# The residual of a transformer layer kept in the result's DRAM rows, with the last norm added by accumulating DMAs

## The chip, the cores and the metric

The kernel runs on 1 core of one Trainium2 chip. The metric is the device time of the program in microseconds; lower is better. Within the core, TensorE (PE) multiplies, VectorE (DVE), ScalarE (ACT) and GpSimd (POOL) do elementwise work, and SyncE (SP) issues DMAs. Each engine takes its instructions strictly in the order of its own queue, and engines wait for each other by semaphores.

## The reference

One layer over x of 1024 tokens by 1024 channels, in float32: a mixing block and a SwiGLU feed-forward block, each with a norm before and after it and a residual around it.

```python
def rms_norm(x, g):
    y = x * lax.rsqrt(jnp.mean(x * x, axis=-1, keepdims=True) + EPS)
    return y * g

def swiglu(h, w1, w2):
    gt, up = jnp.split(h @ w1, 2, axis=-1)
    return (jax.nn.silu(gt) * up) @ w2

h = rms_norm(x, norm_mix_pre)
y = hybrid_mixer(h, ...)                  # four mixers, gates, output projection
x = x + rms_norm(y, norm_mix_post)        # the residual, here called x1
h = rms_norm(x, norm_ffn_pre)
x = x + rms_norm(swiglu(h, w_ffn_in, w_ffn_out), norm_ffn_post)
```

The hidden width of the feed-forward block is 2816. The change concerns how x1 is kept and how the last line adds it.

## The kernel before

Tokens are cut into eight tiles of 128 (rows 0 to 7 below), each 128 partitions by 1024 float32 (512 KB). Products keep float32 accuracy by splitting each operand into a high and a low part (`split`, L139 to L145: ScalarE writes `whi`, VectorE writes `wlo`) and summing three matmuls.

`second_norm` (L1088) computes the residual x1 of each tile and stores it from SyncE into a DRAM tile `x1_{tt}` (L1103, L1105), since SBUF has no room for it during the feed-forward block.

`ffn_out` (L1180) computes the second feed-forward product in three chunks of the hidden width; the third, with `final` true, has three pairs of 128 hidden rows. Each chunk is a Strassen-Winograd scheme of seven products over quadrants. Each product fills four PSUM tiles (`mm_fo`), one for each 128 tokens of a half, and takes 3 pairs times 3 matmuls of 512 columns for each: 36 matmuls. Two sets of four PSUM tiles are used in turns, `ps1` (`mm_fo0` to `mm_fo3`, numbers 1805 to 1808) and `ps2` (`mm_fo4` to `mm_fo7`, numbers 1809 to 1812). `into` (L1266) adds a finished PSUM tile to half of a row's accumulator `ya` (L1272, VectorE). The calls are written in the order of L1319 to L1322: two products, then m6, m5, m3, m7, m4.

- m6, on `ps1`, adds into the first half of rows 4 to 7; m5 goes on in the same PSUM tiles, so it can start only when VectorE has read what m6 left there.
- m3, on `ps1`, completes rows 0 to 3.
- m7, on `ps2`, completes the second half of rows 4 to 7, and m4 goes on in its PSUM tiles and completes rows 4 to 7.

`half_done` (L1278) is the last norm of half a row: the sum of squares on ScalarE (L1282), the multiplication by the norm's weight on VectorE (L1283, in place, so after the square has read), the mean on GpSimd (L1286 for the first half, L1292 for the second), then the reciprocal root on GpSimd (L1294), and for each half of the row `y * r + x1` on VectorE (L1297) and a store of 256 KB from SyncE (L1298). x1 was loaded back into an SBUF slot `x1b` at the first half (L1287 to L1289).

What sets the order: the code is written with priorities (`tc.high_priority`), and a scheduler lays every engine's queue down at build time; slots of SBUF are handed out as earlier tiles die. So an edit can move instructions that it does not name.

Of the kernel before, what the change touches and what calls it, by code (L numbers as in the profile page):

```python
# [9 lines left out]
F32 = mybir.dt.float32  # L10
F32R = mybir.dt.float32r
U8 = mybir.dt.uint8
AF = mybir.ActivationFunctionType
ALU = mybir.AluOpType
# [3 lines left out]
P = 128  # L18
S = 1024
D = 1024  # L20
NT = S // P
# [17 lines left out]
def hybrid_trunk(ctx, tc, x, w_in, w_branch, w_out, w_ffn_in, w_ffn_out, cols, gpost, gfpost,  # L39
                 abias, wst, bsr, wabd, wxbd, lvl, tril, eye, out, dbg=None):  # L40
    nc = tc.nc
    dbg = dbg or {}

    def pool(name, bufs, **kw):
        return ctx.enter_context(tc.tile_pool(name=name, bufs=bufs, **kw))
# [9 lines left out]
    dr = pool("dram", 1, space=bass.MemoryType.DRAM)  # L55
# [24 lines left out]
    def slot(name, dt=F32, w=D):  # L80
        cnt[0] += 1
        t = sp.tile([P, D], dt, tag="S", name=f"{name}_{cnt[0]}", bufs=NSLOT)
        return t[:, :w]
# [17 lines left out]
    def small(name, w):  # L101
        cnt[0] += 1
        return sm.tile([P, w], F32, tag=f"s{w}", name=f"{name}_{cnt[0]}", bufs={1: 24, 8: 8}.get(w, 4))
# [43 lines left out]
    AHEAD_DMA, AHEAD_SUM, AHEAD_OUT, AHEAD_SPLIT = 700, 400, 400, 160  # L147
# [98 lines left out]
    def rstd_of(ss, n, w):  # L246

        ms = small("ms", w)
        nc.gpsimd.tensor_scalar(ms, ss, 1.0 / n, EPS, op0=ALU.mult, op1=ALU.add)
        r = small("rstd", w)  # L250
        last[2] = nc.gpsimd.tensor_tensor(r, ms, neghalf[:, :w], op=ALU.pow)
        return r
# [4 lines left out]
    def halves(name):  # L257

        tiles = {}

        def get(k, ts):
            h = ts.start // 512
            if (h, k // 2) not in tiles:
                tiles[h, k // 2] = slot(f"{name}{h}{k // 2}", F32R)
            b = (k % 2) * 512 - h * 512
            return tiles[h, k // 2][:, b + ts.start : b + ts.stop]

        get.tiles = tiles
        return get
# [97 lines left out]
    def normed(xtile, wait=None):  # L367

        ss = small("ss", 1)
        with after(wait):  # L370
            nc.scalar.activation(junk, xtile, AF.Square, accum_out=ss)
        r = rstd_of(ss, D, 1)
        xn = slot("xn")
        nc.vector.tensor_scalar(xn, xtile, r, None, op0=ALU.mult)
        return xn

    def place_T(srcs, tt, gcol, Th, Tl):

        ts = slice(tt * P, (tt + 2) * P)
        for k in range(0, KT, 2):  # L380
            ps = psmx("tr")
            for v in range(2):
                for u in range(2):
                    nc.tensor.transpose(ps[:, v * 256 + u * P : v * 256 + (u + 1) * P],
                                        srcs[u][:, (k + v) * P : (k + v + 1) * P], ident)
            gs = [cv[:, gcol + k + v : gcol + k + v + 1] for v in range(2)]
            pvs = [ps[:, v * 256 : (v + 1) * 256] for v in range(2)]
            for v in range(2):
                g, pv = gs[v], pvs[v]
                last[0] = nc.scalar.activation(Th(k + v, ts), pv, AF.Copy, scale=g)  # L390
                first_T.append(last[0])
            for v in range(2):
                g, pv = gs[v], pvs[v]
                last[1] = nc.vector.scalar_tensor_tensor(Tl(k + v, ts), pv, g, Th(k + v, ts).bitcast(F32),
                                                         op0=ALU.mult, op1=ALU.subtract)
# [675 lines left out]
    h2h, h2l, x1s = halves("h2h"), halves("h2l"), {}  # L1071
# [16 lines left out]
    def second_norm(th):  # L1088
        xt, xns = {}, {}

        def load(tt):
            xt[tt] = slot("xt2")
            with tc.high_priority(AHEAD_X):
                return nc.sync.dma_start(xt[tt], x[tt * P : (tt + 1) * P, :])

        def residual(tt):
            y = ys.pop(tt)
            ss = small("yss", 1)
            nc.scalar.activation(junk, y, AF.Square, accum_out=ss)
            r = rstd_of(ss, D, 1)  # L1100
            nc.vector.scalar_tensor_tensor(y, y, r, gp, op0=ALU.mult, op1=ALU.mult)
            nc.vector.tensor_tensor(xt[tt], xt[tt], y, op=ALU.add)
            x1s[tt] = dr.tile([P, D], F32, name=f"x1_{tt}")  # L1103
            with tc.issue_after(loads[-1].ins):
                nc.sync.dma_start(x1s[tt], xt[tt])  # L1105

        t0 = 4 * th
        loads = [load(t0 + u) for u in range(4)]
        for u in range(5):
            if u < 4:  # L1110
                residual(t0 + u)
                yield
            if u >= 1:
                xns[u - 1] = normed(xt.pop(t0 + u - 1))
                yield
                if u % 2 == 0:
                    place_T([xns.pop(u - 2), xns.pop(u - 1)], t0 + u - 2, C_GFFN, h2h, h2l)
                    yield
# [61 lines left out]
    def ffn_out(chunk, first, final):  # L1180
        n = len(chunk)
        pairs_ = []
        for i, p in enumerate(chunk):
# [13 lines left out]
            for nm, t in (("A", a), ("B", w)):  # L1197
                for u in range(2):
                    for h in range(2):
                        r, c_ = (h, u) if nm == "A" else (u, h)  # L1200
# [75 lines left out]
        early, xts_ = {}, {}  # L1276

        def half_done(tt, c_, second):  # L1278

            y = yacc[tt][:, halfs[c_]]  # L1280
            ss = small("yss", 1)
            nc.scalar.activation(junk[:, :512], y, AF.Square, accum_out=ss)  # L1282
            nc.vector.tensor_tensor(y, y, gf[:, halfs[c_]], op=ALU.mult)  # L1283
            if not second:
                early[tt] = small("ms0", 1)
                nc.gpsimd.tensor_scalar(early[tt], ss, 1.0 / D, EPS, op0=ALU.mult, op1=ALU.add)  # L1286
                xts_[tt] = slot("x1b")  # L1287
                with tc.high_priority(AHEAD_OUT):
                    nc.sync.dma_start(xts_[tt], x1s[tt])  # L1289
                return  # L1290
            ms = small("ms", 1)
            nc.gpsimd.tensor_scalar(ms, ss, 1.0 / D, early[tt], op0=ALU.mult, op1=ALU.add)  # L1292
            r = small("rstd", 1)
            nc.gpsimd.tensor_tensor(r, ms, neghalf[:, :1], op=ALU.pow)  # L1294
            for cs in (halfs[1 - c_], halfs[c_]):
                xt = xts_[tt][:, cs]
                nc.vector.scalar_tensor_tensor(xt, yacc[tt][:, cs], r, xt, op0=ALU.mult, op1=ALU.add)  # L1297
                nc.sync.dma_start(out[tt * P : (tt + 1) * P, cs], xt)  # L1298
# [4 lines left out]
        def into_last(r, c_, second):  # L1303

            ev = into(r, c_, (r, c_) == (0, 1))

            def evl(t, ps):
                ev(t, ps)
                if final:
                    half_done(4 * r + t, c_, second)  # L1310

            return evl
# [22 lines left out]
    yacc = [slot(f"ya{t}") for t in range(NT)]  # L1335
# [64 lines left out]
```

## Time and profile before

| | |
|---|---|
| median of 3 runs | 1540.26 us (1538.35 to 1542.23) |
| the profiled execution: its own time | 1538.24 us |
| its span in the trace | 1536.4 us |
| PE busy | 1500.5 us, 98% |
| VectorE busy | 1024.8 us, 67% |
| ScalarE busy | 567.6 us, 37% |
| GpSimd busy | 393.9 us, 26% |
| DMAs of the hardware queue | 190.16 MB, 35.5% of 16 engines' span |

The span runs from the first to the last instruction of the trace; 1.84 us of the execution's own time lie around it. A busy PE does not tell what sets the end: in the last stretch of the program the multiplications are over, and the queues of the other engines set it. The views for that are the busy time of each engine by stretch, the instructions in order of time, and the chain of work that ended last. In the lists of instructions a row gives the start, the time until the result is there, the engine, the line, what is written from what, the count, and in brackets the idle time of the engine before it with what ended it. Instructions of one engine overlap a little, so a row's time is some 0.08 us longer than the distance to the next start.

### The profile page before, as it was taken

The numbers are of one execution on the slowest core, as the hardware profiler recorded it, in microseconds if no ns is written. First come the engines' busy times: TensorE is split into PE (matmuls) and PEld (weight loads), VectorE is DVE, ScalarE is ACT, GpSimd is POOL, SyncE is SP. The second block draws the span as 40 slices with busy tenths as digits, with TensorE's granted clock in tenths as the row PEclk, the third lists the DMA queues.
The fourth block names the chain that finished last, engine by engine and source line by source line (L and its number), as shares of the span: only waits on it lengthen the run. The fifth ranks groups of instructions, "written<-read, shape, count | busy, mean of one in ns | idle before, by whom it ended". The sixth has DMA issues, their size and how long they took to land.

```text
span 1536.4 us, 20562 instructions
## 1 busy us (share of the span) xinstructions
PE 1500.5 (98%) x7890; PEld 1253.4 (82%) x7890; DVE 1024.8 (67%) x1569; ACT 567.6 (37%) x942; POOL 393.9 (26%) x343
## 2 busy tenths in 40 slices
PE   8999999999999999999999999999999999999996
PEld 7988888888888878766899978888888888787875
DVE  5986674444459567888765695555555556869898
ACT  6433343333330343344335542222222222553543
POOL 2075333333200100223533223433333330000003
PEclk9999999999999999999999999999999999999998
DMA  6424333333462146563225412222222236630203
GB/s 228 157 85 157 110 110 110 110 110 113 140 213 97 63 157 239 210 243 118 69 97 192 177 64 76 82 85 88 81 84 83 83 110 229 228 112 28 82 22 144
DMA packets 108547, 191.48 MB, mean 125 GB/s; under 512 B 6432, under 2 KB 65440, under 8 KB 108448
## 3 DMA queue, kind: packets, MB, share of 16 engines
q1 hardware_dynamic: 108448, 190.16, 35.5%
q8 instruction: 62, 1.02, 0.3%
q14 instruction: 37, 0.30, 0.1%
HBM read 136.66 MB, written 53.48 MB: 124 GB/s over the span
## 4 chain that ended last, share of the span: by engine, by line
PE 87%; DVE 9%; ACT 2%; issue 1%; POOL 1%; DMA 0%; DVEq 0%; SPq 0%; ACTq 0%; POOLq 0%
PE mm_w L218 16%; PE mm_w L216 16%; PE mm_w L217 16%; PE mm_fo L1239 3%; PE mm_fo L1240 3%; PE mm_fo L1238 3%; PE mm_gate L216 3%; PE mm_gate L217 2%; PE mm_gate L218 2%; PE mm_proj L216 2%; PE mm_proj L217 2%; PE mm_proj L218 2%; PE mm_wo L217 1%; PE mm_wo L218 1%; PE mm_wo L216 1%
## 5 line engine op out<-in xcount | busy, mean ns | idle before, releaser
L142 DVE TENSOR_TENSOR wlo_ws<-s,whi_ws 128x1024 fp32r<-128x1024 f32 x76 | 109.1, 1435 | 54.4 <-ACT whi_ws L141 54.4
L361 DVE TENSOR_TENSOR u<-u,mm_w 128x512 f32<-128x512 f32 x38 | 26.1, 687 | 174.8 <-PE mm_w L218 174.8
L141 ACT CAST whi_ws<-s 128x1024 fp32r<-128x1024 f32 x76 | 80.1, 1054 | 150.2 <-PE mm_w L217 138.3
L1239 PE MATMUL mm_fo<-wlo_fo,whi_fo 128*128 128x512 f32 x308 | 120.2, 392 | 1.3 <-DVE wlo_fo L142 1.3
L1240 PE MATMUL mm_fo<-whi_fo,wlo_fo 128*128 128x512 f32 x308 | 120.2, 392 | 0.1
L324 POOL TENSOR_TENSOR s<-raw_pj 128x512 f32<-128x512 f32 x38 | 57.0, 1500 | 195.7 <-DMA raw_pj<-in_w_in 186.8
L324 POOL TENSOR_TENSOR s<-raw_fu 128x512 f32<-128x512 f32 x19 | 39.7, 2090 | 222.5 <-DMA raw_fu<-in_w_ffn_in 222.5
L1238 PE MATMUL mm_fo<-whi_fo 128*128 128x512 f32 x308 | 91.8, 392 | 4.6 <-DVE ya L1272 3.3
L345 ACT COPY m<-mm_w 128x512 f32<-128x512 f32 x38 | 22.3, 587 | 155.4 <-PE mm_w L218 141.6
L141 ACT CAST whi_fo<-af 128x512 fp32r<-128x512 f32 x66 | 41.2, 624 | 96.4 <-PE mm_fo L1240 76.7
L218 PE MATMUL mm_wo<-whi_wo,ml 128*128 128x256 f32 x256 | 72.4, 284 | 1.2 <-DVE ml L927 1.2
L217 PE MATMUL mm_wo<-wlo_wo,mh 128*128 128x256 f32 x256 | 72.2, 284 | 1.4 <-DVE wlo_wo L142 1.4
L1238 PEld LDWEIGHTS mm_fo<-whi_fo 128*128 128x128 f32 x308 | 57.9, 189 | 19.1 <-DVE ya L1272 4.1
L216 PE MATMUL mm_wo<-whi_wo,mh 128*128 128x256 f32 x256 | 71.5, 284 | 0.6 <-ACT whi_wo L141 0.6
L1239 PEld LDWEIGHTS mm_fo<-wlo_fo,whi_fo 128*128 128x128 f32 x308 | 58.2, 189 | 13.8 <-DVE wlo_fo L142 1.7
L1240 PEld LDWEIGHTS mm_fo<-whi_fo,wlo_fo 128*128 128x128 f32 x308 | 58.2, 189 | 12.6 <-DVE wlo_fo L142 0.4
L1286 POOL TENSOR_SCALAR ms<-yss 128x1 f32<-128x1 f32 x8 | 5.6, 698 | 228.0 <-ACT junk L1282 227.7
L218 PE MATMUL mm_w<-T2h,wlo_ws 128*128 128x512 f32 x152 | 59.3, 390 | 2.2 <-DVE wlo_ws L142 2.2
L217 PE MATMUL mm_w<-T2l,whi_ws 128*128 128x512 f32 x152 | 59.1, 389 | 0.0
L216 PE MATMUL mm_w<-hTh,whi_wa 128*128 128x512 f32 x152 | 59.1, 389 | 0.0
L217 PE MATMUL mm_w<-hTl,whi_wa 128*128 128x512 f32 x152 | 59.1, 389 | 0.0
L216 PE MATMUL mm_w<-T2h,whi_ws 128*128 128x512 f32 x152 | 59.1, 389 | 0.0
(388 smaller groups left out, 4609.2 us busy)
## 6 DMA issues: line engine op xcount, KB each, us to landing
raw_pj<-in_w_in SPq DMA_DIRECT2D x19, 1024.0 KB, 5.9
gt<-st_g SPq DMA_DIRECT2D x22, 512.0 KB, 4.8
raw_fg<-in_w_ffn_in SPq DMA_DIRECT2D x11, 1024.0 KB, 5.1
raw_fu<-in_w_ffn_in SPq DMA_DIRECT2D x11, 1024.0 KB, 5.5
af<-act SPq DMA_DIRECT2D x22, 512.0 KB, 3.9
wf<-in_w_ffn_out SPq DMA_DIRECT2D x18, 512.0 KB, 6.4
xt<-in_x SPq DMA_DIRECT2D x16, 512.0 KB, 7.6
raw_wo<-in_w_out SPq DMA_DIRECT2D x8, 1024.0 KB, 5.1
```

The costliest lines, as they stand in the source:

```text
L141: nc.scalar.copy(hi, src)
L142: return nc.vector.tensor_tensor(lo, src, hi.bitcast(F32), op=ALU.subtract)
L216: nc.tensor.matmul(ps, lhsT=lh(k), rhs=rh(k), start=(not more and k == 0), stop=False, skip_group_check=more)
L217: nc.tensor.matmul(ps, lhsT=lh(k), rhs=rl(k), start=False, stop=False, skip_group_check=more)
L218: nc.tensor.matmul(ps, lhsT=ll(k), rhs=rh(k), start=False, stop=(k == n - 1), skip_group_check=more)
L324: last_sum[0] = nc.gpsimd.tensor_tensor(out_, x0, x1_, op=op)
L345: nc.scalar.copy(m1, p1)
L361: nc.vector.tensor_tensor(u2, u2, p3, op=ALU.add)
L1238: nc.tensor.matmul(ps, lhsT=hi[:, ts], rhs=hi[:, 512:1024], start=start, stop=False, skip_group_check=more)
L1239: nc.tensor.matmul(ps, lhsT=hi[:, ts], rhs=lo[:, 512:1024], start=False, stop=False, skip_group_check=more)
L1240: nc.tensor.matmul(ps, lhsT=lo[:, ts], rhs=hi[:, 512:1024], start=False, stop=stop, skip_group_check=more)
L1286: nc.gpsimd.tensor_scalar(early[tt], ss, 1.0 / D, EPS, op0=ALU.mult, op1=ALU.add)
```

## The change

The stored residual of rows 0 to 6 goes straight into the result's own rows in DRAM; row 7 keeps its DRAM tile. At the end the rows 0 to 6 are not loaded back: ScalarE multiplies the whole row by the reciprocal root in place, and GpSimd issues one DMA of 512 KB that adds it to what stands in the result. Row 7 is done as before.

```diff
-            x1s[tt] = dr.tile([P, D], F32, name=f"x1_{tt}")
+
+            x1s[tt] = dr.tile([P, D], F32, name=f"x1_{tt}") if tt == NT - 1 else out[tt * P : (tt + 1) * P, :]
...
-                xts_[tt] = slot("x1b")
-                with tc.high_priority(AHEAD_OUT):
-                    nc.sync.dma_start(xts_[tt], x1s[tt])
+                if tt == NT - 1:
+                    xts_[tt] = slot("x1b")
+                    with tc.high_priority(AHEAD_OUT):
+                        nc.sync.dma_start(xts_[tt], x1s[tt])
                 return
...
+            if tt < NT - 1:
+                nc.scalar.activation(yacc[tt], yacc[tt], AF.Copy, scale=r)
+                nc.gpsimd.dma_start(x1s[tt], yacc[tt], accum_op=ALU.add)
+                return
             for cs in (halfs[1 - c_], halfs[c_]):
```

Up to the last chunk of `ffn_out` no engine's queue changes but for the target of seven stores. From there on the scheduler lays the queues down differently. Lines from 1104 on are one to six higher in the changed kernel: L1272 is L1273, L1282 is L1283, L1283 is L1284, L1292 is L1294, L1294 is L1296; the new scaling is L1298, the new DMA L1299.

VectorE, at the read of m6's first PSUM tile (`ya4` from `mm_fo0`, entry 1428 of its queue), before:

```order
L142 TENSOR_TENSOR wlo_fo_1872_12640<-wf_1795_12219,whi_fo_1871_12639 128x512
L1272 TENSOR_TENSOR ya3_1672_10990<-ya3_1672_10990,mm_fo7_1812_12246 128x512
L1283 TENSOR_TENSOR ya0_1669_10987<-ya0_1669_10987,gfpost_1668_10985 128x512
L142 TENSOR_TENSOR wlo_fo_1855_12538<-af_1794_12216,whi_fo_1855_12537 128x512
L142 TENSOR_TENSOR wlo_fo_1855_12538<-wf_1796_12220,whi_fo_1855_12537 128x512
L142 TENSOR_TENSOR wlo_fo_1856_12544<-af_1798_12224,whi_fo_1856_12543 128x512
L142 TENSOR_TENSOR wlo_fo_1856_12544<-wf_1800_12228,whi_fo_1856_12543 128x512
L1283 TENSOR_TENSOR ya1_1670_10988<-ya1_1670_10988,gfpost_1668_10985 128x512
L1272 TENSOR_TENSOR ya4_1673_10991<-ya4_1673_10991,mm_fo0_1805_12239 128x512
```

The same read in the changed kernel, now entry 1440:

```order
L1284 TENSOR_TENSOR ya2_1671_10982<-ya2_1671_10982,gfpost_1668_10978 128x512
L142 TENSOR_TENSOR wlo_fo_1874_12629<-wf_1803_12228,whi_fo_1873_12628 128x512
L1284 TENSOR_TENSOR ya3_1672_10983<-ya3_1672_10983,gfpost_1668_10978 128x512
L142 TENSOR_TENSOR wlo_fo_1874_12629<-af_1801_12224,whi_fo_1873_12628 128x512
L142 TENSOR_TENSOR wlo_fo_1886_12697<-af_1794_12209,whi_fo_1885_12696 128x512
L142 TENSOR_TENSOR wlo_fo_1886_12697<-wf_1796_12213,whi_fo_1885_12696 128x512
L142 TENSOR_TENSOR wlo_fo_1889_12703<-af_1798_12217,whi_fo_1888_12702 128x512
L142 TENSOR_TENSOR wlo_fo_1889_12703<-wf_1800_12221,whi_fo_1888_12702 128x512
L142 TENSOR_TENSOR wlo_fo_1892_12709<-af_1802_12225,whi_fo_1891_12708 128x512
L142 TENSOR_TENSOR wlo_fo_1892_12709<-wf_1804_12229,whi_fo_1891_12708 128x512
L1273 TENSOR_TENSOR ya4_1673_10984<-ya4_1673_10984,mm_fo0_1805_12232 128x512
```

The read stands behind four multiplications by the weight instead of two and behind all splits of the last products; on PE all of m7 now stands ahead of m5, where before a few matmuls of m7 stood behind it.

ScalarE, its last entries in the changed kernel (`junk` rows are the squares of half a row, `ya` rows the new scalings; before, the same squares stood there alone):

```order
L1283 ACTIVATE junk_87,yss_1875_12644<-ya4_1673_10984 128x512
L1298 ACTIVATE ya3_1672_10983<-ya3_1672_10983,rstd_1865_12612 128x1024
L1283 ACTIVATE junk_87,yss_1877_12659<-ya5_1674_10985 128x512
L1283 ACTIVATE junk_87,yss_1879_12674<-ya6_1675_10986 128x512
L1283 ACTIVATE junk_87,yss_1881_12689<-ya7_1676_10987 128x512
L1283 ACTIVATE junk_87,yss_1893_12724<-ya4_1673_10984 128x512
L1283 ACTIVATE junk_87,yss_1896_12743<-ya5_1674_10985 128x512
L1298 ACTIVATE ya4_1673_10984<-ya4_1673_10984,rstd_1895_12729 128x1024
L1283 ACTIVATE junk_87,yss_1899_12762<-ya6_1675_10986 128x512
L1298 ACTIVATE ya5_1674_10985<-ya5_1674_10985,rstd_1898_12748 128x1024
L1283 ACTIVATE junk_87,yss_1902_12781<-ya7_1676_10987 128x512
L1298 ACTIVATE ya6_1675_10986<-ya6_1675_10986,rstd_1901_12767 128x1024
```

GpSimd, its last entries in the changed kernel (before, the same entries without the DMAs):

```order
L1299 DMA out_0<-ya4_1673_10984 128x1024
L1294 TENSOR_SCALAR ms_1900_12765<-yss_1899_12762,ms0_1880_12677 128x1
L1296 TENSOR_TENSOR rstd_1901_12767<-ms_1900_12765,neghalf_88 128x1
L1299 DMA out_0<-ya5_1674_10985 128x1024
L1294 TENSOR_SCALAR ms_1903_12784<-yss_1902_12781,ms0_1882_12692 128x1
L1296 TENSOR_TENSOR rstd_1904_12786<-ms_1903_12784,neghalf_88 128x1
L1299 DMA out_0<-ya6_1675_10986 128x1024
```

Each scaling on ScalarE waits for the root of its row from GpSimd, each DMA on GpSimd waits for the scaling of its row, and the mean and the root of row 7 now stand behind the DMA of row 5.

## Rows read from the trace of the kernel before

**Rows 1.** Page: span and busy time of each engine.

```profile
span 1536.4 us, 20562 instructions
PE 1500.5 (98%) x7890; PEld 1253.4 (82%) x7890; DVE 1024.8 (67%) x1569; ACT 567.6 (37%) x942; POOL 393.9 (26%) x343
```

**Rows 2.** Busy time by stretch (columns in the first row); the last row counts matmuls.

```profile
core 0: us, PE busy (x) PEld busy (x) DVE busy (x) ACT busy (x) POOL busy (x), PEclk, DMA share, GB/s
1456.70:1500.00 43.30, 39.92 (x173) 32.16 (x173) 43.29 (x72) 18.54 (x37) 3.04 (x4) 1.00 0.09 31
1509.00:1522.90 13.90, 13.88 (x62) 11.05 (x60) 13.57 (x22) 5.79 (x16) 8.83 (x14) 1.00 0.35 134
1522.90:1533.40 10.50, 0.00 (x0) 0.00 (x0) 10.44 (x17) 2.17 (x6) 5.06 (x7) 0.72 0.44 171
1494.00:1522.90 28.90, 28.88 (x128) 23.45 (x126) 27.09 (x45) 9.95 (x24) 8.83 (x14) 1.00 0.37 137
```

**Rows 3.** Instructions in order of time: PE at m5's start, and its last matmul.

```profile
1493.53 0.50 PE L1238 MATMUL mm_fo<-whi_fo 128*128 128x512 f32 x1 [1.24 <-DVE ya L1272]
1522.49 0.39 PE L1240 MATMUL mm_fo<-whi_fo,wlo_fo 128*128 128x512 f32 x1
```

**Rows 4.** Instructions in order of time: VectorE.

```profile
1456.71 0.69 DVE L142 TENSOR_TENSOR wlo_fo<-af,whi_fo 128x512 fp32r<-128x512 f32 x1 [0.63 <-ACT whi_fo L141]
1492.79 0.68 DVE L1272 TENSOR_TENSOR ya<-ya,mm_fo 128x512 f32<-128x512 f32 x1
1526.22 0.68 DVE L1272 TENSOR_TENSOR ya<-ya,mm_fo 128x512 f32<-128x512 f32 x1
1529.35 1.40 DVE L1297 SCALAR_TENSOR_TENSOR x1b<-ya,rstd,x1b 128x512 f32<-128x512 f32 x2
1531.27 2.07 DVE L1297 SCALAR_TENSOR_TENSOR x1b<-ya,rstd,x1b 128x512 f32<-128x512 f32 x3
```

**Rows 5.** Groups by line, 1509 to 1533.5 us.

```profile
L1297 DVE SCALAR_TENSOR_TENSOR x1b<-ya,rstd,x1b 128x512 f32<-128x512 f32 x16 | 11.4, 744 | 0.3 <-POOL rstd L1294 0.2
L1292 POOL TENSOR_SCALAR ms<-yss,ms 128x1 f32<-128x1 f32 x8 | 6.6, 820 | 22.3 <-ACT junk L1282 22.3
L1294 POOL TENSOR_TENSOR rstd<-ms,neghalf 128x1 f32<-128x1 f32 x8 | 4.8, 599 | 0.7
```

**Rows 6.** Instructions in order of time: ScalarE, squares.

```profile
1516.03 0.63 ACT L1282 ACTIVATE junk<-ya 128x512 f32<-128x512 f32 x1
1516.57 0.19 ACT L1282 ACTIVATION_READ_ACCUMULATOR junk<-ya 128x1 f32 x1
1516.79 0.63 ACT L1282 ACTIVATE junk<-ya 128x512 f32<-128x512 f32 x1
```

**Rows 7.** Groups by line, whole span: ScalarE on a row of 1024, and GpSimd's longest.

```profile
L371 ACT ACTIVATE junk<-xt 128x1024 f32<-128x1024 f32 x16 | 17.2, 1072 | 11.9 <-DVE xt L1102 9.2 <-DMA xt<-in_x 2.6
L494 POOL TENSOR_SCALAR g<-g 128x512 f32<-128x512 f32 x1 | 2.4, 2405 | 0.4 <-DVE g L493 0.4
```

**Rows 8.** SyncE's last stores: duration ns min, median, max; first and last start.

```profile
L1298 SPq DMA_DIRECT2D out<-x1b x16: 332/332/1055, 1511.2 to 1533.4; - x16
```

**Rows 9.** DMA issues: count, KB each, median us from issue to landing.

```profile
x<-xt SPq DMA_DIRECT2D x8, 512.0 KB, 2.7
x1b<-x SPq DMA_DIRECT2D x8, 512.0 KB, 3.7
out<-x1b SPq DMA_DIRECT2D x16, 256.0 KB, 2.0
```

## The prediction

> **What bounds the kernel now.** I read the page first, then the busy time by stretch, then the instructions in order of time of the last 80 us. By the page PE is busy 98% of the span [rows 1], so only what shortens PE's queue or what follows its last matmul can change the time. The stretches show two places where VectorE, not PE, is the late engine. From 1456.7 to 1500 us it is busy 43.29 of 43.30 us while PE has gaps, and from 1522.9 to 1533.4 us it is busy 10.44 of 10.50 us with PE done [rows 2]. In the first of them PE waits for VectorE: m5's first matmul starts at 1493.53 us after 1.24 us of idling, released by the L1272 read that VectorE started at 1492.79 us [rows 3, 4]. PE's last matmul ends at 1522.49 + 0.39 = 1522.88 us [rows 3]. VectorE's last L1297 ends at 1531.27 + 2.07 = 1533.34 us [rows 4], 10.46 us later, and the span ends at 1536.4 us, 3.06 us after that, with the last store, which was issued at 1533.4 us [rows 8]. A store of that kind lands 2.0 us after its issue [rows 9], which leaves 0.9 to 1.0 us behind the landing.
>
> **What is removed.** VectorE loses 14 of 16 instructions on L1297. Three of them in a row take 2.07 us and two 1.40 us [rows 4], so one occupies the queue 0.67 us: 14 x 0.67 = 9.4 us, all in the last VectorE-bound stretch. Seven loads of x1b and 14 stores leave SyncE. I cost them at nothing: where the loads run the DMA share is 0.09 and later at most 0.44 [rows 2], and nothing on SyncE waits behind them. The first store of x1 has the same size and the same queue place as before, so nothing there either.
>
> **The first term: PE ends later.** The removed loads also give SBUF slots back, and the scheduler lays down the last chunk differently. VectorE's read that releases m5 was entry 1428 and is entry 1440. Both queues have the same number of entries up to 1368, which is the split that started at 1456.71 us [rows 4]; from there to 1428 are 60 entries in 1492.79 - 1456.71 = 36.08 us, 0.601 us each, without a gap [rows 2]. So the read starts 12 x 0.601 = 7.2 us later, at 1500.0 us, and m5 follows 0.74 us behind it as now: 1500.75 us. In exchange all of m7 stands ahead of m5, so what is left behind it is m5, m3 and m4, 3 x 36 = 108 matmuls. 128 take 28.9 us [rows 2], so 108 take 24.4 us. The last matmul ends at 1525.15 us: **+2.3 us**. I call this time T.
>
> **The second term: the tail behind T.** The work taken from VectorE goes into two queues that are in order. ScalarE gets seven scalings of 128x1024. The trace has no such Copy; the nearest row on ScalarE reads and writes the same shape in 1.07 us [rows 7], which I take. A square takes 0.76 us from one start to the next [rows 6], a mean 0.82 and a root 0.60 us on GpSimd [rows 5]. How long GpSimd is held by issuing an accumulating DMA no row shows: SyncE's issue takes 0.33 us [rows 8], GpSimd's longest instruction of another kind 2.4 us [rows 7]; I take 1.0 us, nearer to the small one since an issue moves no data, and keep both ends.
>
> Walking the queues in their new order, in us from T (PSUM tiles come 2.04 us apart, rows 0 to 3 at -14.3 to -8.15, rows 4 to 7 at -6.1 to 0):
>
> - Row 0: square ends -12.85, root -11.45, scaling -10.4, DMA issue until -9.4. GpSimd was held, so the means and roots of rows 1 and 2 end at -8.0 and -6.6, the scalings of rows 1 and 2 at -6.95 and -5.5.
> - ScalarE takes row 3's square only now, until -4.75, though its half was there at -7.5; then row 4's first square until -4.0. GpSimd issues the DMAs of rows 1 and 2 until -4.5, row 3's root ends -3.1, its scaling -2.05.
> - Five squares follow on ScalarE: rows 5, 6, 7 first halves, rows 4 and 5 second halves, until 1.75. GpSimd, with the DMA of row 3 and three means between, has the roots of rows 4 and 5 at 2.75 and 4.15.
> - Scaling of row 4 until 3.8, square of row 6 until 4.55, scaling of row 5 until 5.6, square of row 7 until 6.35.
> - GpSimd: DMA of row 4 until 5.15, root of row 6 at 6.55, DMA of row 5 until 7.55, then row 7's mean and root until 8.95. Then VectorE's two L1297 of row 7, 0.67 + 0.74: 10.35.
>
> VectorE ended 10.46 us behind PE and now ends 10.35 us behind it: the 9.4 us it loses come back as ScalarE and GpSimd waiting for each other. Row 7's stores end the span at T + 10.35 + 3.06 = 1538.6 us, **+2.2 us**.
>
> **The third term: the last accumulating DMA.** Row 6's is issued behind row 7's root, at T + 8.95 = 1534.1 us. Its landing is bounded below by a plain store of 512 KB, 2.7 us, and above, as I see it, by a load and a store one after the other, 3.7 + 2.7 = 6.4 us [rows 9]; I take the upper, since each byte has to be read before the sum can be written. With 1.0 us of issue and 0.9 us behind the landing: 1534.1 + 1.0 + 6.4 + 0.9 = 1542.4 us, **+6.0 us**, 3.8 us behind row 7's stores. The DMA share against the rate, 0.44 at 171 GB/s, makes some 390 GB/s, so 512 KB of plain copy occupy the engines 1.35 us, and read twice 2.7 us: about the 2.4 us between the last three issues (4.15, 6.55, 8.95), so I add no queueing.
>
> A page of the Trainium skill speaks against this change here: "Collectives: The Full Stack", section on the bandwidth ceiling, says that an add inside a DMA needs two source reads on one ring and so runs at about half a copy's rate; that would give the same 2.7 us each. No run shows it yet.
>
> **The sum.** 1536.4 + 6.0 = 1542.4 us of span; the profiled execution stands at 1538.24 us, 2.0 us below the median shown, so against the median 1540.26 + 6.0 = **1546.3 us**, 0.4% slower. A measurement of this kernel can tell about 0.3%, 4.6 us, from no change.
>
> **The rivals.**
>
> - *Short landings.* The add is as quick as a plain store, 2.7 us: row 6's lands at 1534.1 + 1.0 + 2.7 + 0.9 = 1538.7 us, level with row 7's stores, and only the first two terms stay: +2.3 us, 1542.6 us. With an issue of 0.33 us four issues on GpSimd's path save 4 x 0.67 = 2.7 us more: 1539.8 us. For it: the DMA engines are less than half busy. The skill's page "DMA: Bandwidth & Descriptors", section on the anatomy of a GpSimd-issued DMA, fits 2.0 us plus bytes over 436 GB/s, an estimate of 3.2 us for 512 KB; by that the sum would be this rival's too. It says nothing of an add, and no row has such a DMA. Chance 0.25.
> - *GpSimd or the DMAs become the bound.* With an issue of 2.4 us four issues on the path (rows 1, 2, 4, 5) and row 6's own add 5 x 1.4 = 7 us: 1553 us. Or the adds queue behind each other: at three times a copy's 1.35 us, 4.05 us each, seven from -9.4 end at T + 19, +10 us, 1550 us; wholly one after the other at 6.4 us they end at T + 35.4, +25 us, 1565 us. For it: these prices are unknown. Against: 16 engines keep many rows in flight. Chance 0.20.
> - *Faster: the tail is freed.* If PE's end does not move and GpSimd's issues are so short that row 3's square starts at -7.5, ScalarE needs 9 squares and 3 scalings, 6.85 + 3.2 = 10.05 us, row 7's square ends at 2.55 and L1297 at 2.55 + 0.82 + 0.60 + 1.41 = 5.4 us, instead of 10.46: 5.1 us faster, 1535.2 us. It decides where an issue holds GpSimd for under some 0.3 us and the adds land within 3 us. For it: 9.4 us do leave the engine that sets the end today. Against: m5's read is 12 entries further back. Chance 0.10.
>
> **How the numbers follow.** The forecast as worked out has 0.45; its own range, landings of 5 to 8 us, is 1544.5 to 1548. From the low edge of the forecast I count 0.05 as no measurable change, so slower by over 0.3% is 0.45 - 0.05 + 0.20 = 0.60; within 0.3% is 0.25 + 0.05 = 0.30, plus nothing of the faster rival; faster 0.10. The range 1538 to 1560 leaves out the faster rival and the far end of the queueing.
>
> **What would show it.** Right: the first matmul of m5 waits for VectorE until some 1500.7 us and PE ends near 1525; VectorE has gaps behind PE's end while ScalarE and GpSimd take turns; row 7's mean starts some 7.5 us behind PE's end, behind row 5's DMA; the last to land is row 6's add. Wrong: PE ending at 1523 or before drops the first term; GpSimd's DMA rows far from 1.0 us change the second; adds that land within 3 us, or each behind the one before, change the third.

## The result and the profile after

The changed kernel takes 1551.51 us (median of 6 runs, 1549.13 to 1553.79); the kernel before, on the same chip, 1541.20 us (6 runs, 1538.35 to 1543.91). The ratio is 1.0068, 95% interval [1.0052, 1.0083]: 0.7% slower, some 10.5 us by the ratio.

The page of the profiled execution of after, which took 1550.66 us; to be set beside [rows 1]:

```profile
span 1548.7 us, 20521 instructions
PE 1506.3 (97%) x7890; PEld 1258.4 (81%) x7890; DVE 1018.4 (66%) x1555; ACT 575.1 (37%) x949; POOL 401.1 (26%) x350
...
q1 hardware_dynamic: 105424, 182.82, 33.9%
q0 software_dynamic: 1008, 3.67, 1.4%
```

VectorE has 14 instructions fewer, ScalarE and GpSimd 7 more each; the queue q0 is new, it carries the seven accumulating DMAs (packets, MB, share of 16 engines' span).

The span is 12.3 us longer. Part of that lies ahead of the change's effect: VectorE's split that began at 1456.71 us in before [rows 4] begins at 1460.86 us, 4.15 us later. Of this, 2.93 us stand ahead of anything that changed: the matmul that starts at 800.03 us in before starts at 802.96 us in after, and the first store of x1 comes only at 828.4 us in before. For the rest, the address of seven stores is the change that could have come in. One kernel's executions spread as widely (beside e1 below, 23 of before ran from 1537.07 to 1543.85 us, and the profiled one took 1538.24), so all profiles below are compared from this split on ("behind the split" counts from its start). The first experiment tests whether that is fair.

After, instructions in order of time on VectorE and PE (start, length, in brackets the idle time ahead and what ended it); against [rows 3, 4]:

```profile
1460.86 0.69 DVE L142 TENSOR_TENSOR wlo_fo<-af,whi_fo 128x512 fp32r<-128x512 f32 x1 [1.42 <-ACT whi_fo L141]
...
1504.17 2.47 DVE L1273 TENSOR_TENSOR ya<-ya,mm_fo 128x512 f32<-128x512 f32 x4
...
1504.90 0.80 PE L1239 MATMUL mm_fo<-whi_fo 128*128 128x512 f32 x1 [3.01 <-DVE ya L1273]
1505.49 0.63 PE L1240 MATMUL mm_fo<-wlo_fo,whi_fo 128*128 128x512 f32 x1
1505.92 0.63 PE L1241 MATMUL mm_fo<-whi_fo,wlo_fo 128*128 128x512 f32 x1
...
1508.62 0.39 PE L1240 MATMUL mm_fo<-wlo_fo,whi_fo 128*128 128x512 f32 x1
1508.85 0.39 PE L1241 MATMUL mm_fo<-whi_fo,wlo_fo 128*128 128x512 f32 x1
...
1530.63 0.39 PE L1241 MATMUL mm_fo<-whi_fo,wlo_fo 128*128 128x512 f32 x1
```

The read that releases m5 starts 1504.17 - 1460.86 = 43.31 us behind the split, where it started 36.08 us behind it before: 7.23 us later. m5 follows after PE has idled 3.01 us instead of 1.24. Then something new shows: m5's first matmuls start 0.43 us apart, later ones 0.23 us. PE ends at 1531.02 us, 70.16 us behind the split; before it was 66.17.

After, busy time by stretch, same columns as [rows 2]:

```profile
1460.90:1500.00 39.10, 36.92 (x159) 29.33 (x158) 39.10 (x66) 21.70 (x42) 7.02 (x3) 1.00 0.04 14
1500.00:1510.00 10.00, 6.98 (x23) 4.97 (x23) 9.21 (x16) 0.11 (x1) 4.49 (x2) 0.83 0.00 0
1510.00:1525.00 15.00, 15.00 (x68) 12.42 (x67) 8.84 (x14) 4.33 (x9) 4.53 (x7) 1.00 0.15 22
1525.00:1536.00 11.00, 6.02 (x27) 4.66 (x25) 7.09 (x12) 9.13 (x21) 7.80 (x14) 0.96 0.93 162
1531.00:1540.60 9.60, 0.02 (x1) 0.00 (x0) 6.12 (x10) 6.46 (x13) 7.40 (x13) 0.71 0.90 160
1536.00:1548.70 12.70, 0.00 (x0) 0.00 (x0) 2.52 (x4) 2.44 (x4) 3.81 (x7) 0.50 0.83 166
```

The reader is to see three things. The granted clock is 0.83 in the ten microseconds in which m5 starts. Behind PE's end VectorE is no longer full: from 1531.00 to 1540.60 us, the stretch from PE's end to VectorE's, it is busy 6.12 of 9.60 us, where it was 10.44 of 10.50 [rows 2]. And the DMA engines are nearly full: a share of 0.90 at 160 GB/s in that stretch (0.93 from 1525 to 1536 us), where before 0.44 moved 171 GB/s.

After, the last instructions in order of time:

```profile
1537.23 0.90 POOL L1299 DMA_DIRECT2D out<-ya  x1
1537.30 1.15 ACT L1298 ACTIVATE ya<-ya,rstd 128x1024 f32<-128x1024 f32 x1
1537.37 0.69 DVE L1284 TENSOR_TENSOR ya<-ya,gfpost 128x512 f32<-128x512 f32 x1 [0.96 <-ACT junk L1283]
1537.90 0.55 POOL L1294 TENSOR_SCALAR ms<-yss,ms 128x1 f32<-128x1 f32 x1
1538.53 0.57 POOL L1296 TENSOR_TENSOR rstd<-ms,neghalf 128x1 f32<-128x1 f32 x1
1539.06 0.91 POOL L1299 DMA_DIRECT2D out<-ya  x1
1539.14 1.42 DVE L1303 SCALAR_TENSOR_TENSOR x1b<-ya,rstd,x1b 128x512 f32<-128x512 f32 x2 [1.07 <-POOL rstd L1296]
1539.92 1.00 SPq L1304 DMA_DIRECT2D out<-x1b  x2
```

After, the adding line's view: its issues (duration in ns, min/median/max, first and last start) and their landing; against [rows 8]:

```profile
L1299 POOL DMA_DIRECT2D out<-ya x7: 862/909/1077, 1521.3 to 1539.1; - x7
...
DMA to landing us min/median/max: 5.4/6.2/8.0
```

After, the DMA view from 1518 to 1549 us: q0's share of the engines; then, by the storing line's view, row 7's plain stores with their landing; against [rows 8, 9]:

```profile
q0 software_dynamic: 1008, 3.67, 69.4%
```

```profile
L1304 SPq DMA_DIRECT2D out<-x1b x2: 338/340/343, 1539.9 to 1540.6; - x2
...
DMA to landing us min/median/max: 7.1/7.2/7.3
```

Row 7's mean stands behind row 5's DMA, VectorE ends 9.54 us behind PE (10.46 before), and the span ends 17.68 us behind PE (13.52 before). The seven adds take 69.4% of 16 engines over 31 us, 3.07 us of all 16 each. The last to land is not row 6's add: issued at 1539.1 us, it lands within 8.0 us, by 1547.1 us. Row 7's two stores of 256 KB, issued into that stream, land 7.2 us after their issue instead of 2.0, the second at 1540.6 + 7.1 = 1547.7 us, and the span ends some 1.0 us behind that.

From the split on, then: 70.16 - 66.17 = 4.0 us of later PE end, and 17.68 - 13.52 = 4.2 us behind it, 8.2 us together, at the lower edge of what the ratio says (8.0 to 12.8 us).

### The profile page after: what moved, and what is told of

Read it like the earlier page. It is cut to its first block, busy times and chain, and to the rows that moved or that the text cites. A ratio compares the mean times of both kernels' runs of the same rounds, so it can differ in the third digit from the quotient of the medians.

```text
span 1548.7 us, 20521 instructions
## 1 busy us (share of the span) xinstructions
PE 1506.3 (97%) x7890; PEld 1258.4 (81%) x7890; DVE 1018.4 (66%) x1555; ACT 575.1 (37%) x949; POOL 401.1 (26%) x350
## 4 chain that ended last, share of the span: by engine, by line
PE 86%; DVE 9%; ACT 2%; issue 2%; POOL 1%; DMA 1%; DVEq 0%; SPq 0%; ACTq 0%; POOLq 0%
PE mm_w L218 16%; PE mm_w L217 15%; PE mm_w L216 15%; PE mm_fo L1240 3%; PE mm_fo L1241 3%; PE mm_fo L1239 3%; PE mm_gate L216 2%; PE mm_gate L218 2%; PE mm_gate L217 2%; PE mm_proj L216 2%; DVE wlo_fo L142 2%; PE mm_wo L217 1%; PE mm_wo L218 1%; PE mm_wo L216 1%; PE mm_proj L217 1%
## 5 line engine op out<-in xcount | busy, mean ns | idle before, releaser
L361 DVE TENSOR_TENSOR u<-u,mm_w 128x512 f32<-128x512 f32 x38 | 26.1, 687 | 174.4 <-PE mm_w L218 174.4
L1287 POOL TENSOR_SCALAR ms<-yss 128x1 f32<-128x1 f32 x8 | 12.6, 1580 | 227.0 <-ACT junk L1283 226.7
```

Source lines behind the costliest of these rows:

```text
L361: nc.vector.tensor_tensor(u2, u2, p3, op=ALU.add)
```

## The experiments

Theory A: about half of the loss is PE's later end, by the order that the freed slots bring, and half is what lands behind it because of the adds; the 4 us ahead of the split are variation. The rivals are stated with each kernel. The table holds what every profile shows, one profile for each kernel, in us: PE's end behind the split, VectorE's last L1297 (L1303) behind PE's end, the span's end behind PE's end; and the ratio to before from all runs, with before run beside each kernel.

| kernel | PE end - split | VectorE end - PE end | span end - PE end | ratio [95%] |
|---|---|---|---|---|
| before | 66.17 | 10.46 | 13.5 | |
| after | 70.16 | 9.54 | 17.7 | 1.0068 [1.0052, 1.0083] |
| e1 store target alone | 66.18 | 10.47 | 13.5 | 1.0003 [0.9991, 1.0015] |
| e2 seven adds, order held | 66.15 | 8.73 | 17.9 | 1.0037 [1.0022, 1.0052] |
| e3 plain stores, GpSimd | 70.42 | 8.94 | 12.8 | 1.0038 [1.0026, 1.0050] |
| e4 plain stores, SyncE | 70.43 | 8.59 | 12.7 | 1.0025 [1.0009, 1.0040] |
| e5 row 6 alone | 66.18 | 9.68 | 15.9 | 1.0019 [1.0009, 1.0030] |
| e6 rows 0 to 3 | 67.04 | 10.15 | 13.3 | 1.0012 [1.0003, 1.0021] |
| e7 rows 2, 3, order held | 66.17 | 8.42 | 11.5 | 0.9984 [0.9973, 0.9995] |
| e8 rows 2, 4 | 65.54 | 8.71 | 14.3 | 1.0005 [0.9995, 1.0015] |
| e9 e2 scaling on VectorE | 66.13 | 8.04 | 18.7 | 1.0032 [1.0020, 1.0043] |

### e1: the store target alone

The kernel before, with the one changed line of `residual`:

```diff
-            x1s[tt] = dr.tile([P, D], F32, name=f"x1_{tt}")
+            x1s[tt] = dr.tile([P, D], F32, name=f"x1_{tt}") if tt == NT - 1 else out[tt * P : (tt + 1) * P, :]
```

> Only the place of x1 changes: rows 0 to 6 are stored into the result's rows and loaded back from there; norm, adds and loads are those of before. In the profile of after, everything was 4.15 us late at the split that began at 1456.71 us before, long ahead of the last chunk, and only this part of the change lies ahead of that place. Theory A (that lateness is variation from one execution to the next): no difference, 1541 us within 2 us, PE's end and the tail as before. Rival C (the new target of the stores costs time in the middle of the kernel): 2 to 4 us slower, 1543 to 1545 us, and the profile late by 1456.7 us.

No difference that the runs can tell: 1.0003, at most 2.3 us by the interval. Its profile: VectorE's split, PE's last matmul and VectorE's last L1297 in order of time, then, by stretch, 800 to 1000 us in e1 and, below it, in before:

```profile
1459.91 0.69 DVE L142 TENSOR_TENSOR wlo_fo<-af,whi_fo 128x512 fp32r<-128x512 f32 x1 [0.63 <-ACT whi_fo L141]
...
1525.70 0.39 PE L1240 MATMUL mm_fo<-whi_fo,wlo_fo 128*128 128x512 f32 x1
...
1534.49 2.07 DVE L1297 SCALAR_TENSOR_TENSOR x1b<-ya,rstd,x1b 128x512 f32<-128x512 f32 x3
```

```profile
800.00:1000.00 200.00, 195.92 (x1135) 174.26 (x1135) 126.49 (x169) 80.70 (x137) 63.15 (x52) 0.98 0.33 115
```

```profile
800.00:1000.00 200.00, 195.92 (x1145) 173.15 (x1144) 126.69 (x171) 81.26 (x138) 63.34 (x52) 1.00 0.33 115
```

This execution too has the split 3.2 us late, with a granted clock of 0.98 in a stretch that has 1.00 in before's profile; from the split on it is before's to 0.01 us. So a profile can be that late without the ratio moving. e9, whose stores of x1 go where after's go, gains nothing between a matmul at 800 us and one at 1100 us (1.97 and 2.00 us later than in before). And before's own runs differ in the same way: of the 35 beside e5 to e8, those under 1538.4 us list a granted clock of 0.996 to 0.997, those over 1543 us 0.993 to 0.994. The lateness ahead of the split is variation between executions that goes with the clock, and rival C falls. The profiles of e1 to e9 all have the split 2 to 5 us later than before's, which was a quick execution.

### e2: all seven adds, the order held

After, but every row keeps its slot and its load of `x1b` (the loaded rows 0 to 6 are not used); the scaling writes into that slot:

```diff
-                if tt == NT - 1:
+                if True:
                     xts_[tt] = slot("x1b")
...
-                nc.scalar.activation(yacc[tt], yacc[tt], AF.Copy, scale=r)
-                nc.gpsimd.dma_start(x1s[tt], yacc[tt], accum_op=ALU.add)
+                nc.scalar.activation(xts_[tt], yacc[tt], AF.Copy, scale=r)
+                nc.gpsimd.dma_start(x1s[tt], xts_[tt], accum_op=ALU.add)
```

> All seven adds as in after, but the loads of x1b and their SBUF slots are kept (the loaded rows are not used; ScalarE writes the scaled rows into those slots instead of in place). VectorE's queue up to the read that releases m5 is then that of before. Theory A (half of the loss is PE's later end, by the order, the other half the adds behind it): m5 waits some 1.2 us as before, PE ends 4.0 us earlier than in after when both are measured from the split at 1456.7 us (2.6 us of it the read, 1.4 us the lower clock), the adds still end some 4 us later behind PE's end than the stores of before did: 1545 us, 4 us over before, 6 us under after's 1551.5. Rival B (the adds and GpSimd's queue alone make the loss, PE's end is hidden under them): 1549 to 1552 us.

1.0037, 1545.89 us: theory A's 1545, below rival B's 1549 to 1552. Its split, m5's first matmul and PE's last, VectorE's last L1303 in order of time:

```profile
1460.03 0.69 DVE L142 TENSOR_TENSOR wlo_fo<-af,whi_fo 128x512 fp32r<-128x512 f32 x1 [0.63 <-ACT whi_fo L141]
...
1496.85 0.50 PE L1239 MATMUL mm_fo<-whi_fo 128*128 128x512 f32 x1 [1.26 <-DVE ya L1273]
...
1525.79 0.39 PE L1241 MATMUL mm_fo<-whi_fo,wlo_fo 128*128 128x512 f32 x1
...
1533.49 1.42 DVE L1303 SCALAR_TENSOR_TENSOR x1b<-ya,rstd,x1b 128x512 f32<-128x512 f32 x2 [1.07 <-POOL rstd L1296]
```

With the slots held, m5 starts 36.82 us behind the split, as before, the granted clock from 1500 to 1510 us is 1.00, and PE ends 4.0 us earlier than in after. The tail keeps its length, 17.9 us against 17.7. The order and the adds are two separate losses, and the order's is worth the 0.3% between the two ratios.

### e3 and e4: the adds replaced by plain stores

Both leave the residual out of rows 0 to 6; e3 stores from GpSimd, e4 from SyncE:

```diff
-                nc.gpsimd.dma_start(x1s[tt], yacc[tt], accum_op=ALU.add)
+                nc.gpsimd.dma_start(x1s[tt], yacc[tt])
```

```diff
-                nc.gpsimd.dma_start(x1s[tt], yacc[tt], accum_op=ALU.add)
+                nc.sync.dma_start(x1s[tt], yacc[tt])
```

> After with plain stores on GpSimd's queue in place of the accumulating ones: the residual is left out of rows 0 to 6. Order, scaling and GpSimd's issues stay. Theory A (the add itself lands late): PE's end stays as in after; row 6's store is issued some 8.0 us behind it and lands in 2.7 to 3.5 us, so that row 7's stores end the span, some 12.6 us behind PE's end instead of 17.7: 5 us under after, 1546.5 us, 5 us over before. Rival D (any DMA that GpSimd issues lands in 6 to 8 us, add or not): as after, 1550 to 1552 us.

> After with plain stores of the scaled rows issued by SyncE (0.33 us each there): the residual is left out of rows 0 to 6, GpSimd issues nothing. Order and scaling stay. Theory A (four issues of 0.9 to 1.1 us hold GpSimd's roots in the tail): the last L1303 ends some 7.5 us behind PE's end instead of 9.5, the span some 10.5 us behind it; with PE's end 4 us later than before the sum is 1541 + 4 - 3 = 1542 us. Rival E (the issues on GpSimd cost nothing, ScalarE's scalings and squares alone set the tail): the last L1303 stays at 9.5 us, span 12.6 us behind PE's end, 1546 us, no difference from the kernel with plain stores on GpSimd's queue.

e3, the storing line's view, issues and landing, and then q0 on its page:

```profile
L1299 POOL DMA_DIRECT2D out<-ya x7: 531/617/783, 1520.3 to 1537.5; - x7
...
DMA to landing us min/median/max: 2.9/3.0/3.3
```

```profile
q0 software_dynamic: 1008, 3.67, 0.6%
```

The same bytes through the same queue land in 3.0 us instead of 6.2 and take 0.6% of the engines instead of 1.4%. PE ends as late as in after, the span ends 12.8 us behind it instead of 17.7: 4.9 us are what adding costs over storing. Theory A said 1546.5 us, the runs 1544.9; rival D, that any DMA issued by GpSimd lands so late, falls.

e4 was to end another 2 us sooner, and did not. VectorE's last waits in its tail, in order of time:

```profile
1535.22 0.69 DVE L1284 TENSOR_TENSOR ya<-ya,gfpost 128x512 f32<-128x512 f32 x1 [1.31 <-ACT junk L1283]
1536.87 0.69 DVE L1284 TENSOR_TENSOR ya<-ya,gfpost 128x512 f32<-128x512 f32 x1 [0.96 <-ACT junk L1283]
...
1538.36 1.41 DVE L1303 SCALAR_TENSOR_TENSOR x1b<-ya,rstd,x1b 128x512 f32<-128x512 f32 x2 [0.80 <-POOL rstd L1296]
```

VectorE waits for the squares as it does in e3, and its last L1303 ends 8.59 us behind PE's end against 8.94. So e3's issues on GpSimd cost 0.35 us, not 2, and the longer ones of the adds 0.95 us (9.54 against 8.59): with nothing issued on GpSimd, VectorE still waits for ScalarE's squares, which stand between the scalings. Theory A was wrong in this part, rival E right in substance; the intervals of e3 and e4 overlap.

### e5: one late add alone

Rows 0 to 5 keep slot, load and the two L1297, as row 7 does; the x1 store and the `x1b` load are divided by the same condition:

```diff
-            if tt < NT - 1:
+            if tt in (6,):
```

> Only row 6 is scaled on ScalarE and added by an accumulating DMA; rows 0 to 5 and 7 are as before. VectorE's queue up to the read that releases m5 is that of before, so PE should end as before. Theory A (a lone add lands as quickly as the quickest of the seven, 5.3 us, and those of 8 us queue behind others): its issue stands some 7.5 us behind PE's end, so it lands at 7.5 + 0.9 + 5.3, with 0.9 us behind it 14.6 us behind PE's end, where the span of before ended 13.5 us behind it: 1 us slower, 1541 to 1542 us. Rival F (8 us whatever else runs): 17.3 us behind PE's end, 4 us slower, 1543 to 1545 us.

1.0019, some 3 us. Its one issue stands at 1535.73 us, 8.18 us behind PE's end, and takes 1.07 us. The landing by the adding line's view, that of row 7's two stores by theirs, and q0 by the DMA view from 1520 to 1545 us:

```profile
DMA to landing us min/median/max: 6.0/6.0/6.0
```

```profile
DMA to landing us min/median/max: 5.2/5.3/5.4
```

```profile
q0 software_dynamic: 144, 0.52, 13.3%
```

Alone, the add lands in 6.0 us and takes 13.3% of 25 us, 3.3 us of all 16 engines. The time, 1543.69 us, is in rival F's range, but not for its reason: 15.9 us behind PE's end lies between 14.6 and 17.3, and the add lands in 6.0 us, neither 5.3 nor 8. Here too row 7's stores are the last to land, the second at 1542.5 us, 0.7 us behind the add. A lone add needs 6 us; the 8.0 us of after's slowest, and what e2 has beyond 15.9, are what the other adds put on top.

### e6, e7, e8: adds for a few rows

All three take the condition as in e5, with `(0, 1, 2, 3)`, `(2, 3)` and `(2, 4)`; e7 also keeps all loads and slots, as e2 does.

> Rows 0 to 3 as in after (result's rows, scaling on ScalarE, accumulating DMA, no load of x1b and no slot for it), rows 4 to 7 as before. Their adds are issued before PE's end or close to it. Theory A: the adds cost nothing here, since they have landed when row 7's stores go; the slots of four rows are free, so the order moves in part and m5 starts about 1 us later than in before; the tail behind PE's end is about half a microsecond shorter than 13.5 us: 0 to 2 us slower. Rival B (adds and GpSimd's queue alone make the loss, whichever rows they are): 3 to 6 us slower.

> Rows 2 and 3 alone by scaling and accumulating DMA, with all loads of x1b and their slots kept, so the order up to m5 is that of before and PE ends as before. VectorE loses four L1297 (2.7 us) in the stretch in which it sets the end, ScalarE and GpSimd get two scalings and two issues, both before PE's end. Theory A (a few early rows free VectorE without making ScalarE and GpSimd take turns at the end): the last L1297 ends some 2 us earlier behind PE's end, 1537 to 1538.5 us, about 0.15% faster than before, at the edge of what the rounds can tell. Rival G (ScalarE's chain of squares and scalings takes VectorE's place at once): no difference or up to 2 us slower.

> Rows 2 and 4 alone by scaling and accumulating DMA, without loads or slots for them. The order moves slightly: m5 does not start later than in before. Theory A: VectorE's last L1297 ends some 2.6 us earlier behind PE's end than in before; row 4's add is issued some 2.5 us behind PE's end and lands 6 us later, just before row 7's stores: 2 to 3 us faster than before, 1537 to 1539 us, 0.2%. Rival G: ScalarE's chain delays rows 5 to 7, or row 4's add lands last: no difference or slower by up to 3 us.

e6 came out at 1.0012: PE's end 0.87 us later, with the slots of four rows freed, and a tail 0.2 us shorter. Adds that land before row 7's stores cost next to nothing; rival B falls a second time.

e7, its split, PE's last matmul and VectorE's end:

```profile
1460.47 0.69 DVE L142 TENSOR_TENSOR wlo_fo<-af,whi_fo 128x512 fp32r<-128x512 f32 x1 [0.63 <-ACT whi_fo L141]
...
1526.25 0.39 PE L1241 MATMUL mm_fo<-whi_fo,wlo_fo 128*128 128x512 f32 x1
...
1532.99 2.07 DVE L1303 SCALAR_TENSOR_TENSOR x1b<-ya,rstd,x1b 128x512 f32<-128x512 f32 x3
```

PE ends as in before, VectorE 2.0 us sooner behind it, the span as well: 0.9984, 2.5 us faster than before. The interval, 0.8 to 4.2 us, only just leaves out no change; that the profile's 2.0 us agree is what speaks for a real gain. So the idea of the change seems to work, a little, for two rows whose scalings ScalarE takes early and whose adds have landed before the last stores come.

e8 was to gain as much and gained nothing, 1.0005. Its DMA view from 1520 to 1545 us, and the stretch from 1532 to 1536 us:

```profile
out<-x1b SPq DMA_DIRECT2D x8, 256.0 KB, 4.4
out<-ya POOLq DMA_DIRECT2D x2, 512.0 KB, 6.5
```

```profile
1532.00:1536.00 4.00, 0.00 (x0) 0.00 (x0) 1.66 (x3) 0.00 (x0) 0.00 (x0) 0.50 1.02 332
```

VectorE ends 8.71 us behind PE, 1.75 us sooner than before where 2.6 were foreseen, and PE ends 0.6 us sooner. But row 4's add, issued at 1527.83 us, takes 7.4 us to land, beside the last rows' plain stores, and these land in 4.4 us (the median) instead of 2.0, with the DMA engines full. The gain is handed back behind VectorE's end: 14.3 - 8.7 = 5.5 us where before had 3.1. That is rival G's outcome, though it is the stores behind the add that land last, not the add.

### e9: the scaling on VectorE

e2 with one line changed:

```diff
-                nc.scalar.activation(xts_[tt], yacc[tt], AF.Copy, scale=r)
+                nc.vector.tensor_scalar(xts_[tt], yacc[tt], r, None, op0=ALU.mult)
```

> As the kernel with all seven adds and the order held (its last L1303 ended 8.7 us behind PE's end, its span 17.9 us), but the seven scalings of 128x1024 run on VectorE instead of ScalarE. Theory H (ScalarE's queue of squares and scalings is what ate most of the 9.4 us that left VectorE): ScalarE is free for row 3's to row 7's squares, VectorE has two thirds of its old work back, adds are issued earlier; the last L1303 ends 6 to 8 us behind PE's end, the span 15 to 17 us behind it: 1542 to 1545 us. Rival I (it makes no difference which of the two scales, because VectorE then makes GpSimd and the adds wait as long): the last L1303 ends 9 to 10.5 us behind PE's end, the adds 18 to 20.5 us: 1546 to 1549 us.

Its scalings by their line's view (ns, min/median/max), then the last issues and VectorE's end in order of time, then row 7's stores by the DMA view from 1512 to 1545 us:

```profile
L1298 DVE TENSOR_SCALAR x1b<-ya,rstd x7: 735/740/782, 1512.4 to 1529.7; 128x1024 f32<-128x1024 f32 x7
```

```profile
1531.16 1.99 POOL L1299 DMA_DIRECT2D out<-x1b  x2
1531.43 1.41 DVE L1303 SCALAR_TENSOR_TENSOR x1b<-ya,rstd,x1b 128x512 f32<-128x512 f32 x2 [0.94 <-POOL rstd L1296]
```

```profile
out<-x1b SPq DMA_DIRECT2D x2, 256.0 KB, 8.3
```

The scaling takes 0.74 us here, against 1.13 to 1.15 on ScalarE. VectorE ends 8.04 us behind PE, at the edge of theory H and sooner than rival I had it; the span ends 18.7 us behind PE, as rival I said, and the time is 1546.39 us. H falls where it matters: VectorE ends 0.7 us sooner than in e2, the span 0.8 us later. From 1531.5 to 1541.9 us the share of the DMA engines is 0.92 here, and in e2 as well. So with all seven adds it is their stream through the DMA engines that sets the end, whichever engine scales.

## Why the prediction was right, and what it mis-sized

The sign and the wide range held: 1546.3 us was forecast, in 1538 to 1560, against 1551.5. The forecast's own range, 1544.5 to 1548, with a chance of 0.45, was missed. The time is near the 1550 and 1553 us of the rival in which GpSimd or the DMAs become the bound; but half of the loss is PE's end, so neither of these prices was met by its reason. The steps, one by one:

- *Stores of x1 in another place, removed loads and stores: nothing.* Right for the place, by e1. For the loads it agrees with e2, in which all seven still run and the tail is as long as in after; at PE's end loads and order were only changed together.
- *PE's end, +2.3 us.* The mechanism is shown by e2, and its first half hit: 12 queue entries made the releasing read 7.23 us later, against 7.2 foreseen. The 108 matmuls behind it were priced at 24.4 us from a stretch at full clock, but took 1531.02 - 1504.90 = 26.1 us. By m5's rows, the first seven matmuls take 1.4 us more than at the later spacing: PE had stood for 3.0 us and came back at the lower level. The term was 4.0 us; the forecast was 1.7 us short, 1.4 of it by the clock.
- *The tail: 9.4 us leave VectorE and come back as waits.* Right in the sum: 9.54 us behind PE's end against 10.35 foreseen, with 1.0 us taken for an issue and 0.86 to 1.08 measured. The 9.4 us do not all leave the stretch behind PE's end, as the prediction says: before, 7 of the 14 L1297 end ahead of it. And who holds whom was half wrong, so that the sum was in part lucky. The walk made GpSimd's issues four steps of the path; e4 takes them away and gains 0.35 us over e3, 0.95 us over after. What VectorE waits for there is ScalarE's queue of squares and scalings, and by e9 even that is not what ends the span.
- *The last add, +6.0 us with the terms before it.* The issue came 8.04 us behind PE's end (8.95 foreseen). "I add no queueing" is the step that failed. The last three adds were issued 1.85 and 1.83 us apart, not 2.4, and each fills the engines for 3.07 us. By that the third should take 2 x 1.23 = 2.5 us more to land than the first, an estimate; they land in 5.5, 6.2 and 8.0 us. Row 7's stores, which the walk had ending 3.06 us behind VectorE and 3.8 us ahead of the add, take 7.2 us and land last, in after as in e5. So the sign "the last to land is row 6's add" was wrong. The span ended 9.64 us behind the start of the last issue, not 8.3. That the miss is no larger is also luck: the rows count a landing from the start of its issue, so the prediction's 1.0 + 6.4 us is to be set against 6.0 us for a lone add (e5) and 8.0 us for after's slowest.
- *What a byte costs.* The forecast's 2.7 us of all engines for a 512 KB add was 3.07 in after; e3's plain stores took 35.9% of 25 us over seven, 1.28 us. The half rate that the Trainium skill's page "Collectives: The Full Stack" gives, in its section on the bandwidth ceiling, for the adding step of a ReduceScatter ring, where the add needs two source reads on one ring, is borne out in kind: here an add took 2.4 times a copy's engine time. Why it is more than twice, no run here shows.

The sum from the split on is 4.0 + 4.2 = 8.2 us. It lies within the interval of the ratio's 10.5 us, near its lower end. In e3 the profile from the split on gives 4.3 - 0.8 = 3.5 us, just under the ratio's 4.0 to 7.7 us. So some 2 us may stand ahead of the split or come from single executions; what they are is not settled.

The rivals: *short landings* fell: 5.4 us was the quickest in after, 5.2 us in any run. The fit of the page "DMA: Bandwidth & Descriptors" of the Trainium skill, section on the anatomy of a GpSimd-issued DMA, estimated 3.2 us for 512 KB; that agrees with e3's plain copies (2.9 to 3.3 us) and not with adds. *The DMAs become the bound* was right in kind: the adds fill the engines and the last landings queue. Its 1565 us was far too high, since the adds share the engines and do not follow each other whole, and three times a copy was 2.4. Its 1550 us is also not what its own sum gives: seven times 4.05 us from T - 9.4 end at T + 19, with 0.9 us behind the landing 8.6 us over before, not 10, some 1549 us. The other half, an issue of 2.4 us on GpSimd, did not come: 0.86 to 1.08 us. *Faster: the tail is freed* asked that PE's end stay; e2 gives it that, and VectorE still ends 8.73 us behind PE, not 5.4, with the adds behind it. What the rival saw shows for two early rows (e7), as far as 0.16% can show it.

## What to carry to other kernels

In this kernel an accumulating DMA takes work off an engine and puts 2.4 times a copy's load on the DMA engines: use it where its landing is covered and no last plain store runs beside it, so for early rows. Freeing buffers is an edit to the order too; look at which read releases the next matmul before counting an unneeded load as a gain, and keep the slot if the old order was better. Where PE is made to wait longer, price the matmuls that follow at the clock they will get, not at that of an undisturbed stretch.

## What was not expected of the hardware

- After PE's wait of 3.0 us the granted clock was 0.83 from 1500 to 1510 us, and matmuls of 512 columns started 0.43 us apart, near twice 0.23, the lower of the two levels, 1.2 against 2.4 GHz. e3 and e4, with the same order, show 0.83 there as well. Before and e2, whose waits around this place are 2.0 and 1.2 to 1.3 us, show 1.00 there, and so does e6, where m5 starts 5.4 us later behind the split than in before, but after a wait of only 1.2 us.
- A GpSimd issue of an accumulating DMA took 0.86 to 1.08 us in after and up to 1.40 us in e9, of a plain one 0.53 to 0.78 us in e3.
- Plain stores of 256 KB landed in 2.0 us in before, 2.7 behind seven plain stores (e3), 4.4 and 5.3 beside one add (e8, e5) and 7.2 to 8.3 behind seven (after, e2, e9); all are medians. In after and e5, row 7's second store landed 0.6 and 0.7 us behind the last add, though issued 1.5 us after it.
- VectorE scaled 128x1024 in 0.74 us, about as long as one L1297 of 128x512 [rows 5]; ScalarE took 1.13 to 1.15 us.
